# Delta rule in a decoder layer: substitution on 128 blocks of 16 rows instead of 64 of 32, one more doubling by products, one DMA per head each way, and other assumed durations in the planner

## The chip, the cores and the metric

The kernel runs on one core of one Trainium2 chip. The metric is the device time in microseconds of one execution on that core, as the median of several runs. TensorE is called PE in the profile, VectorE DVE, ScalarE ACT, GpSimd POOL and SyncE SP; PEld is TensorE's loading of weights, and SPq is the queue in which SP issues its DMAs.

## The reference

One layer of a decoder: a SwiGLU feed-forward network, a mixer of two head groups, a cross-attention to 256 memory tokens, and a second feed-forward network, over 512 tokens of width 1024, all in float32. The change is in the second head group of the mixer, the gated delta rule (4 heads of 128). Cut to what matters:

```python
L = where(strict, einsum('bhncd,bhnsd->bhncs', k_beta, k) * decay, 0.0)
A = L + eye(CHUNK)
u = triangular_solve(A, v_beta, left_side=True, lower=True)
w = triangular_solve(A, k_beta * exp(g)[..., None], left_side=True, lower=True)
attn_intra = einsum('bhncd,bhnsd->bhncs', q, k) * decay

def step(state, xs):                       # over the chunks
    w_c, u_c, qd_c, a_c, kt_c, gl_c = xs
    v_new = u_c - w_c @ state
    o = qd_c @ state + a_c @ v_new
    state = state * exp(gl_c) + kt_c.T @ v_new
    return state, o
```

The kernel works with chunks of 128 tokens, four per head, which give the same output. So for each head and chunk it needs the inverse of a unit lower triangular matrix I + L of 128 rows; T is that inverse, X its transpose.

## The kernel before

The feed-forward networks and projections are products of a [128 x 512] moving operand; every float32 weight block comes by DMA as `raw` (three buffers), ScalarE writes its high part `wh`, VectorE or GpSimd its low part `wl` (four buffers each), and TensorE makes three products of the parts. These are the "wide products" with `xt` and `wh` or `wl` in their names. In the mixer GpSimd makes the low part of every second block.

The order in which the engines issue is not the order of the code. The class `Issue` keeps every instruction with what it reads and writes, gives each an assumed duration (`add`, lines 119 to 183), and at the end (`settle`, line 226) places them on their engines, forwards and backwards by turns, the most urgent of those ready first. Each engine and SP's queue then issue in that order. Every instruction is recorded in one helper, so the profile shows one line, L270, for nearly all, and the names of tiles tell them apart.

The delta rule runs in these steps. The gates (`gw`, `yd`, `gc`) are worked out by token on VectorE, from a transpose of `zr` on TensorE. For each head the keys are convolved (`cy`, `cth`, `co`), transposed and multiplied (`kk`) to give `L` (lines 962 to 989). Then the diagonal blocks of 32 rows of all heads, 4 heads x 4 chunks x 4 blocks = 64, go through DRAM: `L` of a head is stored to `dl`, and four DMAs, one per chunk, load its blocks into `Lb` with a block to a partition. The substitution (lines 992 to 998) runs on 64 partitions for all heads at once, in `Tb`, which begins as the identity:

```python
for j in range(31):
    n = [64, 31 - j, j + 1]
    w_ = Wb[0:64, 0 : n[1] * n[2]].rearrange("p (r s) -> p r s", s=n[2])
    V.tensor_tensor(w_, Lb[:, j + 1 :, j : j + 1].to_broadcast(n), Tb[:, j : j + 1, 0 : j + 1].to_broadcast(n), ALU.mult)
    V.tensor_tensor(Tb[:, j + 1 :, 0 : j + 1], Tb[:, j + 1 :, 0 : j + 1], w_, ALU.subtract)
```

In `inverse` (line 1038), for each head, four DMAs store the blocks to `dt`, which holds zeros elsewhere, and one loads them as `T`; VectorE flips `T` to `X`. Small products then double the blocks twice, from 32 to 64 and from 64 to 128 rows: `L` times `X` into `Qs`, then `T` times `Qs` into `X` and, where the next doubling needs it, `T`. Then `qv` makes queries and values (`aT`, `vb`, `qe`), and `scan` runs over the four chunks. `PLAN` (line 29) orders these steps in the code, with `fox_values` (the values of the other head group, weights `wmn`) among them; it decides PSUM banks and buffers, and the planner's order follows from data and buffers. Behind the scans come the other head group's attention pairs.

## Time and profile before

| | |
|---|---|
| time of three runs | 1222.79, 1224.2, 1224.33 us; median 1224.2 |
| span of the profiled execution | 1222.4 us |
| TensorE busy | 1192.9 us, 98% |
| VectorE busy | 642.7 us, 53% |
| ScalarE, GpSimd busy | 493.0 us (40%), 128.6 us (11%) |
| chain of work that ended last | TensorE 87%, VectorE 7%, DMA 2% |
| mean granted clock of TensorE | 0.995 of full speed |

The span runs from the first instruction to the last of one execution; a run's time lies 1.8 us above it at the median, for what lies around it. Busy time is the union of an engine's instructions. The idle time of an engine is put down to what ended it. The granted clock is a share of full speed: 1.0 is 2.4 GHz, and where a stretch shows less, TensorE ran at 1.2 GHz for part of it.

### The profile page before, as it was taken

The page shows a single profiled execution, that of the slowest core. Times are in us where ns is not written, and L with a number is a line of the kernel's source. Part 1 is how long each engine was busy: PE and PEld are TensorE (multiplying, and loading weights), DVE is VectorE, ACT ScalarE, POOL GpSimd, SP SyncE. Part 2 cuts the span into 40 slices and gives each one's busy share as a digit, 9 for nine tenths or more (in the row PEclk, how much of TensorE's full clock was granted, in tenths as well). Part 3 has the DMA queues.
Part 4 walks back from the last instruction along what each step waited for, and adds up shares of the span by engine and source line. Part 5 has one row for each costly group of instructions (what it writes and reads, how often), then busy time and mean ns, then how long its engine had stood idle before and what let it go on. Part 6 is the DMA issues. An engine that isn't in the chain of part 4 may idle for free.

```text
span 1222.4 us, 15630 instructions
## 1 busy us (share of the span) xinstructions
PE 1192.9 (98%) x6078; PEld 1002.6 (82%) x6078; DVE 642.7 (53%) x1152; ACT 493.0 (40%) x1024; POOL 128.6 (11%) x121
## 2 busy tenths in 40 slices
PE   7999999999999899899999999999999999999997
PEld 7888888888888687788787888888988888888886
DVE  5655455442327979469975744546634334342323
ACT  5323223222226564368974644435422323222221
POOL 1000000000001432222020442012000000000000
PEclk9999999999999999999999999999999999999999
DMA  5332322333333231211214253222432332333321
GB/s 192 122 100 90 103 88 102 103 103 104 109 101 104 87 113 57 91 54 54 73 60 164 91 181 118 79 67 65 125 103 88 102 97 93 104 107 100 102 71 69
DMA packets 41753, 120.32 MB, mean 98 GB/s; under 512 B 9424, under 2 KB 9680, under 8 KB 41680
## 3 DMA queue, kind: packets, MB, share of 16 engines
q1 hardware_dynamic: 41168, 119.20, 30.9%
q8 instruction: 47, 0.77, 0.3%
q0 software_dynamic: 512, 0.13, 0.1%
q14 instruction: 26, 0.21, 0.1%
HBM read 114.73 MB, written 4.46 MB: 98 GB/s over the span
## 4 chain that ended last, share of the span: by engine, by line
PE 87%; DVE 7%; DMA 2%; issue 2%; ACT 2%; SPq 0%; POOL 0%; DVEq 0%; POOLq 0%; ACTq 0%
PE psum L270 87%; DVE Wb L270 1%; DVE Tb L270 1%; DMA mr<-in_mem_dram 1%; DVE wl L270 1%; DVE gw L270 1%; DMA raw<-in_wkvk_dram 1%; DVE co L270 1%; DVE xn L270 1%; DVE cy L270 0%; SPq L270 0%; DMA h<-in_x_dram 0%; DVE smalls L270 0%; DVE pt L270 0%; DVE h L270 0%
## 5 line engine op out<-in xcount | busy, mean ns | idle before, releaser
L270 PE MATMUL psum<-xt,wh 128*128 128x512 f32 (+1 forms) x2064 | 599.4, 374 | 0.3 <-ACT wh L270 0.2
L270 PEld LDWEIGHTS psum<-xt,wh 128*128 128x128 f32 x2064 | 373.6, 190 | 63.5 <-ACT wh L270 0.5
L270 ACT ACTIVATE wh<-raw 128x1024 fp32r<-128x1024 f32 (+1 forms) x202 | 213.0, 1056 | 526.0 <-PE psum L270 293.3
L270 PE MATMUL psum<-xt,wl 128*128 128x512 f32 (+1 forms) x1016 | 376.6, 375 | 0.8 <-DVE wl L270 0.7
L270 DVE TENSOR_TENSOR wl<-raw,wh 128x1024 fp32r<-128x1024 f32 (+1 forms) x176 | 216.3, 1230 | 275.8 <-ACT wh L270 275.2
L270 PEld LDWEIGHTS psum<-xt,wl 128*128 128x128 f32 x1016 | 190.9, 190 | 32.7 <-DVE wl L270 1.2
L270 PE MATMUL psum<-wh,hh 128*128 128x512 f32 x352 | 137.1, 390 | 0.0
L270 PE MATMUL psum<-wl,hh 128*128 128x512 f32 x352 | 137.1, 390 | 0.0
L270 PE MATMUL psum<-wh,hl 128*128 128x512 f32 x352 | 137.0, 389 | 0.0
L270 POOL TENSOR_TENSOR smalls<-smalls,mhalf 128x1 f32<-128x1 f32 (+1 forms) x38 | 26.5, 700 | 789.8 <-ACT smalls L270 784.0
L270 PEld LDWEIGHTS psum<-wh,hh 128*128 128x128 f32 x352 | 66.1, 188 | 13.8
L270 PEld LDWEIGHTS psum<-wh,hl 128*128 128x128 f32 x352 | 66.1, 188 | 13.6
L270 PEld LDWEIGHTS psum<-wl,hh 128*128 128x128 f32 x352 | 66.1, 188 | 13.6
L270 POOL TENSOR_TENSOR wl<-raw,wh 128x1024 fp32r<-128x1024 f32 x26 | 63.7, 2450 | 120.8 <-ACT wh L270 110.2
L270 PE MATMUL psum<-wh,xt 128*128 128x512 f32 x128 | 43.5, 409 | 0.4 <-DVE q L270 0.4
L270 DVE SCALAR_TENSOR_TENSOR hv<-s,psum 128x512 f32<-128x512 f32 x22 | 15.1, 688 | 53.7 <-PE psum L270 53.5
L270 DVE TENSOR_TENSOR tu<-psum,rb 128x512 f32<-128x512 f32 x22 | 15.2, 692 | 53.4 <-PE psum L270 53.3
L270 DVE TENSOR_TENSOR fg<-psum,gbc 128x512 f32<-128x512 f32 x32 | 22.0, 688 | 37.1 <-ACT u L270 37.1
L270 DVE TENSOR_TENSOR tg<-psum,rb 128x512 f32<-128x512 f32 x22 | 15.2, 692 | 44.5 <-PE psum L270 44.5
L270 ACT ACTIVATE u<-psum 128x512 f32<-128x512 f32 x32 | 19.0, 593 | 41.4 <-PE psum L270 41.4
L270 ACT ACTIVATE hh<-hv 128x512 fp32r<-128x512 f32 x44 | 27.4, 623 | 16.2 <-DVE hv L270 16.2
L270 DVE TENSOR_TENSOR hl<-hv,hh 128x512 fp32r<-128x512 f32 x44 | 30.1, 685 | 1.5 <-ACT hh L270 1.5
(232 smaller groups left out, 1431.3 us busy)
## 6 DMA issues: line engine op xcount, KB each, us to landing
raw<-in_f2gu_dram SPq DMA_DIRECT2D x44, 512.0 KB
raw<-in_f1gu_dram SPq DMA_DIRECT2D x43, 512.0 KB
raw<-in_f1d_dram SPq DMA_DIRECT2D x22, 512.0 KB
raw<-in_f2d_dram SPq DMA_DIRECT2D x22, 512.0 KB
raw<-in_wmt_dram SPq DMA_DIRECT2D x21, 512.0 KB
gbc<-in_gains_dram SPq DMA_DIRECT2D x16, 256.0 KB
raw<-in_wmn_dram SPq DMA_DIRECT2D x8, 512.0 KB
raw<-in_wout_dram SPq DMA_DIRECT2D x8, 512.0 KB
```

What stands on the lines that cost most here:

```text
L270: r = call(*args, **kw)
```

## The change

The blocks of the substitution have 16 rows, 128 of them, one on each partition, and it has 15 steps. A new doubling from 16 to 32 rows by products comes first: for each head 16 products `L` times `X`, a mask (`low16`, new columns of the constant `cr`) on the way from PSUM, 16 + 12 products with `Qs`, and seven subtractions on VectorE. The blocks of a head move with one DMA each way instead of four, in a layout of the DRAM buffers by chunks, with runs of 64 bytes instead of 128. `Lb` and `Tb` have 256 columns instead of 1024, `Wb` has a tile of its own, and there are 54 slots instead of 51. In the planner's assumed durations a float32r product costs 10.7 ns more, a float32 product on at most 32 rows half as much, and a `tensor_tensor_scan` 2.04 ns a column. Comments are gone as well, so the helper's line is now L273.

```diff
-NSLOT = 51
+NSLOT = 54
...
-            cost = max(size * passes * 0.41667, cols * 0.8333) + 2.6
+            cost = max(size * passes * 0.41667, cols * 0.8333) + (13.3 if passes == 1 else 2.6)
+            if passes == 4 and rows <= 32:
+                cost /= 2
...
-            cost = 68 + size * (6.3 if op == "reciprocal" else 0.521 if single else 1.042) + 61 * scalars
+            each = {"reciprocal": 6.3, "tensor_tensor_scan": 2.04}.get(op, 0.521 if single else 1.042)
+            cost = 68 + size * each + 61 * scalars
...
-    NB = 32 * S + 32
+    NB = 16 * P + 16
+    NC = 8 * NB
     def rows_of(buf):
-        return buf.rearrange("b x -> (b x)")[0 : P * S].rearrange("(p q) -> p q", q=S)
-    def blocks_of(buf, c):
-        return buf[:, 0 : 32 * S].rearrange("b (r q) -> b r q", q=S)[:, :, c * P : c * P + 32]
+        return buf.rearrange("c (p q) -> p c q", q=P)[0:P]
+    def blocks_of(buf):
+        flat = buf.rearrange("c x -> (c x)").rearrange("(i x) -> i x", x=NB)
+        return flat[:, 0 : 16 * P].rearrange("i (r q) -> i r q", q=P)[:, :, 0:16]
...
-        Q.dma_start(rows_of(dl[hh]), L)
-        for c in range(NT):
-            p0 = 16 * hh + 4 * c
-            Q.dma_start(Lb[p0 : p0 + 4], blocks_of(dl[hh], c))
+        Q.dma_start(rows_of(dl[hh]), by_chunk(L))
+        Q.dma_start(Lb[32 * hh : 32 * hh + 32], blocks_of(dl[hh]))
...
-    for j in range(31):
-        n = [64, 31 - j, j + 1]
-        w_ = Wb[0:64, 0 : n[1] * n[2]].rearrange("p (r s) -> p r s", s=n[2])
+    for j in range(15):
+        n = [P, 15 - j, j + 1]
+        w_ = Wb[:, 0 : n[1] * n[2]].rearrange("p (r s) -> p r s", s=n[2])
...
-        for c in range(NT):
-            p0 = 16 * hh + 4 * c
-            Q.dma_start(blocks_of(dt_[hh], c), Tb[p0 : p0 + 4])
+        Q.dma_start(blocks_of(dt_[hh]), Tb[32 * hh : 32 * hh + 32])
         T = u(s="T", ring=gr)
-        Q.dma_start(T, rows_of(dt_[hh]))
+        Q.dma_start(by_chunk(T), rows_of(dt_[hh]))
...
+        quarters = [slice(32 * i, 32 * i + 32) for i in range(4)]
+        qp = pg()
+        for c in range(NT):
+            for b in quarters:
+                mm(qp[b, 32 * c : 32 * c + 32], ck(L, c)[b, b], ck(X, c)[b, b], start=True, stop=True)
+        V.tensor_tensor(c3(Qs[:, 0:P]), c3(qp[:, 0:P]), low16[:, None, :].to_broadcast([P, NT, 32]), ALU.mult)
+        xp = pg()
+        for c in range(NT):
+            for b in quarters:
+                mm(xp[b, 32 * c : 32 * c + 32], ck(T, c)[b, b], Qs[b, 32 * c : 32 * c + 32], start=True, stop=True)
+            for b in quarters[0:3]:
+                mm(xp[b, P + 32 * c : P + 32 * c + 32], Qs[b, 32 * c : 32 * c + 32], ck(T, c)[b, b], start=True, stop=True)
+        for i, b in enumerate(quarters):
+            V.tensor_tensor(c3(X)[b, :, b], c3(X)[b, :, b], c3(xp[:, 0:P])[b], ALU.subtract)
+            if i < 3:
+                V.tensor_tensor(c3(T)[b, :, b], c3(T)[b, :, b], c3(xp[:, P : 2 * P])[b], ALU.subtract)
```

The change moves instructions on every engine. Three places show it; the numbers in the names tell buffers apart.

TensorE at the first product with X, before. `wh_4046` and `wh_4076` are weights of the values of the other head group:

```order
L270 MATMUL psum<-wh_4046,xt_2564 128x512
L270 MATMUL psum<-wh_4046,xt_2563 128x512
L270 MATMUL psum<-wl_4047,xt_2563 128x512
L270 MATMUL psum<-wh_4046,xt_2564 128x512
L270 MATMUL psum<-X_3692,L_3092 32x32 x4
L270 MATMUL psum<-wh_4076,xt_2563 128x512
L270 MATMUL psum<-wl_4077,xt_2563 128x512
L270 MATMUL psum<-wh_4076,xt_2564 128x512
```

And the same place after; `wh_3928` and `wh_3968` are the query and value weights of the last head:

```order
L273 MATMUL psum<-xt_2563,wl_3929 128x512
L273 MATMUL psum<-cm_2736 128x512
L273 MATMUL psum<-ao_3012,ao_3008 128x128 x4
L273 MATMUL psum<-xt_2561,wh_3968 128x512
L273 MATMUL psum<-X_3787,L_3141 32x32 x16
L273 MATMUL psum<-xt_2562,wh_3968 128x512
L273 MATMUL psum<-xt_2561,wl_3969 128x512
L273 MATMUL psum<-xt_2561,wh_3968 128x512
L273 MATMUL psum<-Qs_3789,T_3785 32x32 x4
L273 MATMUL psum<-T_3785,Qs_3789 32x32 x2
L273 MATMUL psum<-X_3645,L_3092 32x32 x13
```

The first product with X stood behind three of the four blocks of the other group's values; now it stands ahead of all four and inside the last head's projections, and two heads' small products follow each other.

VectorE from the end of the substitution to the flips of `T`, before:

```order
L270 TENSOR_TENSOR Wb_3048<-Lb,Tb 64x31
L270 TENSOR_TENSOR Tb<-Tb,Wb_3048 64x31
L270 TENSOR_TENSOR wl_4374<-raw_4371,wh_4373 128x1024
L270 STREAM_TRANSPOSE X_3692<-T_3690 128x512
L270 STREAM_TRANSPOSE X_3785<-T_3783 128x512
```

And after:

```order
L273 TENSOR_TENSOR Wb<-Lb,Tb 128x15
L273 TENSOR_TENSOR Tb<-Tb,Wb 128x15
L273 TENSOR_TENSOR wl_4071<-raw_4068,wh_4070 128x1024
L273 SCALAR_TENSOR_TENSOR co_3568<-cth_3562,cy_3560 128x512
L273 SCALAR_TENSOR_TENSOR cy_3600<-psum,cw,cy_3600 128x511
L273 TENSOR_TENSOR aT_3528<-psum,Dt_3517 128x512
L273 SCALAR_TENSOR_TENSOR cy_3600<-psum,cw,cy_3600 128x510
L273 STREAM_TRANSPOSE X_3787<-T_3785 128x512
L273 STREAM_TRANSPOSE X_3645<-T_3643 128x512
```

Five instructions, not one, stand between the last step and the first flip.

SP's queue on the way back, before; `raw` from `in_wmt` are weights of the attention pairs:

```order
L270 DMA raw_4329<-in_wmt_dram 128x1024
L270 DMA raw_4371<-in_wmt_dram 128x1024
L270 DMA raw_4568<-in_wmt_dram 128x1024
L270 DMA dt_3036<-Tb 4x32x32 x4
L270 DMA dt_3037<-Tb 4x32x32 x4
L270 DMA dt_3038<-Tb 4x32x32
L270 DMA T_3690<-dt_3036 128x512
L270 DMA dt_3038<-Tb 4x32x32 x3
L270 DMA T_3783<-dt_3037 128x512
L270 DMA dt_3039<-Tb 4x32x32 x4
L270 DMA raw_4610<-in_wmt_dram 128x1024
```

And after:

```order
L273 DMA raw_4128<-in_wmn_dram 128x1024
L273 DMA dt_3037<-Tb 32x16x16
L273 DMA dt_3036<-Tb 32x16x16
L273 DMA dt_3039<-Tb 32x16x16
L273 DMA dt_3038<-Tb 32x16x16
L273 DMA T_3785<-dt_3037 128x4x128
L273 DMA T_3643<-dt_3036 128x4x128
L273 DMA raw_4481<-in_wmt_dram 128x1024
L273 DMA raw_4523<-in_wmt_dram 128x1024
L273 DMA raw_4720<-in_wmt_dram 128x1024
```

Nine stores stood ahead of the first load of `T`, now four do, and the weights of the attention pairs moved from ahead of the stores to behind the loads.

## Rows read from the trace of the kernel before

**Rows 1.** The page, busy time by engine: share of the span, instructions.

```profile
PE 1192.9 (98%) x6078; PEld 1002.6 (82%) x6078; DVE 642.7 (53%) x1152; ACT 493.0 (40%) x1024; POOL 128.6 (11%) x121
```

**Rows 2.** TensorE in time: start, us, operation [idle before, what ended it].

```profile
410.80 1.08 PE L270 MATMUL psum<-ident,yd 128*128 128x128 f32 x4 [4.05 <-DVE smalls L270]
...
463.13 0.49 PE L270 MATMUL psum<-cm 128*128 128x512 f32 x1 [2.63 <-ACT vb L270]
...
502.32 0.52 PE L270 MATMUL psum<-X,L 32*32 32x32 f32 x8 [3.28 <-DVE X L270]
```

**Rows 3.** Stretches: length, PE, PEld, DVE, ACT, POOL busy, granted clock, DMA.

```profile
396.00:501.55 105.55, 95.10 (x482) 77.86 (x481) 90.89 (x182) 56.15 (x147) 36.76 (x24) 0.97 0.27 82
396.00:410.80 14.80, 10.75 (x75) 9.76 (x75) 14.33 (x28) 7.55 (x19) 7.08 (x4) 0.99 0.43 133
464.00:470.00 6.00, 6.00 (x23) 4.82 (x23) 5.90 (x11) 3.95 (x9) 1.10 (x1) 0.72 0.13 11
502.00:506.00 4.00, 3.68 (x15) 2.54 (x15) 0.97 (x2) 0.53 (x2) 0.60 (x1) 0.57 0.64 180
...
502.30:544.00 41.70, 41.64 (x402) 34.07 (x402) 23.01 (x63) 23.50 (x84) 7.21 (x9) 0.96 0.27 84
```

**Rows 4.** Stretches, the instructions with Wb alone: length, DVE busy, clock, DMA.

```profile
440.00:500.00 60.00, 29.96 (x62) 0.97 0.22 66
```

**Rows 5.** VectorE in time: three steps of the substitution, the last one with it.

```profile
449.72 0.21 DVE L270 TENSOR_TENSOR Tb<-Tb,Wb 64x60 f32<-64x60 f32 x1
...
457.39 2.46 DVE L270 TENSOR_TENSOR Wb<-Lb,Tb 64x207 f32<-64x207 f32 x1
...
492.53 2.41 DVE L270 TENSOR_TENSOR Tb<-Tb,Wb 64x31 f32<-64x31 f32 x1
```

**Rows 6.** GpSimd in time, at the second of those steps.

```profile
457.11 2.50 POOL L270 TENSOR_TENSOR wl<-raw,wh 128x1024 fp32r<-128x1024 f32 x1
```

**Rows 7.** TensorE in time: wide products one behind another.

```profile
497.06 0.39 PE L270 MATMUL psum<-wl,xt 128*128 128x512 f32 x1
...
497.74 0.39 PE L270 MATMUL psum<-wl,xt 128*128 128x512 f32 x1
```

**Rows 8.** Groups by form, 396 to 502 us: busy us, mean ns | idle before.

```profile
L270 DVE TENSOR_TENSOR wl<-raw,wh 128x1024 fp32r<-128x1024 f32 x8 | 10.1, 1264 | 0.0
...
L270 DVE SCALAR_TENSOR_TENSOR co<-cth,cy 128x512 f32<-128x512 f32 x11 | 9.3, 844 | 3.7 <-ACT cth L270 3.7
...
L270 DVE SCALAR_TENSOR_TENSOR cy<-psum,cw,cy 128x511 f32<-128x511 f32 x11 | 8.2, 745 | 1.8 <-ACT cth L270 1.7
```

**Rows 9.** The chain that ended last, 492 to 512 us: start, us, what.

```profile
494.96 0.27 SPq L270
...
498.87 2.65 DMA T<-dt
...
501.55 0.72 DVE X L270
```

**Rows 10.** SP's queue in time: a store of L, a load that waits.

```profile
428.07 0.33 SPq L270 DMA_DIRECT2D dl<-L  x1
...
430.42 0.67 SPq L270 DMA_DIRECT2D Lb<-dl  x2
```

**Rows 11.** Groups by form, 502 to 544 us: the first doubling's products.

```profile
L270 PE MATMUL psum<-X,L 32*32 32x32 f32 x64 | 3.4, 196 | 3.3 <-DVE X L270 3.3
```

**Rows 12.** TensorE in time: two groups of small products.

```profile
527.06 0.40 PE L270 MATMUL psum<-xt,wh 128*128 128x512 f32 x1
527.39 0.43 PE L270 MATMUL psum<-X,L 32*32 32x32 f32 x8
527.75 0.50 PE L270 MATMUL psum<-xt,wh 128*128 128x512 f32 x1
...
528.80 0.21 PE L270 MATMUL psum<-X,L 32*32 32x32 f32 x1
...
528.91 0.32 PE L270 MATMUL psum<-X,L 32*32 32x32 f32 x5
```

More of the change, by code (lines that the diff above doesn't have):

```diff
@@ L304, in tile_decoder_layer @@
     crow: bass.AP,
-    cid32: bass.AP,
+    cid16: bass.AP,
     out: bass.AP,
@@ L728, in tile_decoder_layer @@
     identR, mstrict, minclT, mdiag = (cm[:, i * P : (i + 1) * P] for i in range(4))
-    cr = issue.tile(pool, [P, 11], F32, tag="cr", name="cr")
+    cr = issue.tile(pool, [P, 43], F32, tag="cr", name="cr")
     QK.dma_start(cr, crow)
@@ L748, in tile_decoder_layer @@
     sel = cr[:, 7:11]
+    low16 = cr[:, 11:43]
     w_first = [wblock(wmt[i]) for i in range(4)]
@@ L895, in tile_decoder_layer, with by_chunk @@
         move("m", r_, n_)
-    NB = 32 * S + 32
+    NB = 16 * P + 16
+    NC = 8 * NB
     def rows_of(buf):
-        return buf.rearrange("b x -> (b x)")[0 : P * S].rearrange("(p q) -> p q", q=S)
-    def blocks_of(buf, c):
-        return buf[:, 0 : 32 * S].rearrange("b (r q) -> b r q", q=S)[:, :, c * P : c * P + 32]
-    dl = [issue.tile(dram, [4, NB], F32, tag="dl", bufs=4, name=nm("dl"), grain=(0, 32)) for _ in range(GH)]
-    dt_ = [issue.tile(dram, [4, NB], F32, tag="dt", bufs=4, name=nm("dt"), grain=(0, 32)) for _ in range(GH)]
+        return buf.rearrange("c (p q) -> p c q", q=P)[0:P]
+    def blocks_of(buf):
+        flat = buf.rearrange("c x -> (c x)").rearrange("(i x) -> i x", x=NB)
+        return flat[:, 0 : 16 * P].rearrange("i (r q) -> i r q", q=P)[:, :, 0:16]
+    dl = [issue.tile(dram, [4, NC], F32, tag="dl", bufs=4, name=nm("dl"), grain=(0, NC)) for _ in range(GH)]
+    dt_ = [issue.tile(dram, [4, NC], F32, tag="dt", bufs=4, name=nm("dt"), grain=(0, NC)) for _ in range(GH)]
+    def by_chunk(t_):
+        return t_.rearrange("p (c q) -> p c q", c=NT)
     zb = u(s="zb")
@@ L910, in tile_decoder_layer @@
     for hh in range(GH):
-        Q.dma_start(rows_of(dt_[hh]), zb)
+        Q.dma_start(rows_of(dt_[hh]), by_chunk(zb))
     fr(zb)
-    Lb, Tb = (issue.tile(pool, [P, D], F32, tag=t_, name=t_, grain=(4, 1024))[0:64].rearrange("p (r s) -> p r s", r=32) for t_ in ("Lb", "Tb"))
-    Wb = u(s="Wb")
-    QK.dma_start(Tb, cid32.rearrange("p (r s) -> p r s", r=32))
+    Lb, Tb = (
+        issue.tile(pool, [P, 256], F32, tag=t_, name=t_, grain=(32, 256)).rearrange("p (r s) -> p r s", r=16)
+        for t_ in ("Lb", "Tb")
+    )
+    Wb = issue.tile(pool, [P, 64], F32, tag="Wb", name="Wb")
+    QK.dma_start(Tb, cid16.rearrange("p (r s) -> p r s", r=16))
     def banks(hh):
@@ L1066, in inverse @@
             for c in range(NT):
-                mm(xp[up, 32 * c : 32 * c + 32], ck(T, c)[up, up], Qs[up, 32 * c : 32 * c + 32], start=True, stop=True)
+                mm(xp[up, 32 * c : 32 * c + 32], ck(T, c)[up, up], Qs[up, P + 32 * c : P + 32 * c + 32], start=True, stop=True)
                 if i == 0:
@@ L1070, in inverse @@
                         xp[dn, P + 32 * c : P + 32 * c + 32],
-                        Qs[up, 32 * c : 32 * c + 32],
+                        Qs[up, P + 32 * c : P + 32 * c + 32],
                         ck(T, c)[up, up],
@@ L1460, in _consts @@
     cmask = np.concatenate([ident, mstrict, minclT, mdiag], axis=1)
-    crow = np.zeros((P, 11), np.float32)
+    crow = np.zeros((P, 43), np.float32)
     crow[:, 0:1] = np.where(r % 16 < 4, 1.0, -1.0)
@@ L1471, in _consts @@
         crow[32 * m, 7 + m] = 1.0
-    cid32 = np.ascontiguousarray(np.broadcast_to(np.eye(32, dtype=np.float32).reshape(1, 1024), (64, 1024)))
-    return cmask, crow, cid32
+    crow[:, 11:43] = (r % 32 < 16) & (np.arange(32)[None, :] >= 16)
+    cid16 = np.ascontiguousarray(np.broadcast_to(np.eye(16, dtype=np.float32).reshape(1, 256), (P, 256)))
+    return cmask, crow, cid16
 def kernel(**inputs):
@@ L1535 @@
     )
-    cmask, crow, cid32 = _consts(np)
+    cmask, crow, cid16 = _consts(np)
     arrs = dict(
@@ L1558 @@
         crow=crow,
-        cid32=cid32,
+        cid16=cid16,
     )
```

6 lines of the change are left out of this document (2 added, 4 removed).

## The prediction

> **What bounds the kernel now.** I read the page first. TensorE is busy for 98% of the span [rows 1], so the time is TensorE's work plus its waits (the few us before its first and behind its last product aside), and a change counts only by what it adds to that work or takes from those waits. The second view is TensorE's instructions in time, with the idle time ahead of each. From 400 to 503 us three rows carry waits of over 2 us: 4.05 us ahead of the gates' transposes, 2.63 us ahead of a mask product, and 3.28 us ahead of the first doubling product, which waits for X [rows 2]. The last two, 5.9 us, fall while the substitution runs or just behind it. The third view is the stretches. From 396.00 to 501.55 us, from the gates' transposes to the flip that makes the first X, VectorE is busy for 90.89 of 105.55 us and TensorE for 95.10; behind the last two waits the granted clock is 0.72 for 6 us and 0.57 for 4 us [rows 3]. At the lower of the two levels (1.2 instead of 2.4 GHz for part of each stretch) TensorE loses 6 x 0.28 = 1.7 us and 4 x 0.43 = 1.7 us, the second partly while idle, say 1.6. So the lateness of VectorE costs 5.9 + 3.3 = 9.2 us at these two places. This is what the change can reach there.
>
> Why is VectorE late? The substitution takes 29.96 us of it, 62 instructions [rows 4]. A step of 60 columns takes 0.21 us when undisturbed; one of 207 columns took 2.46 us [rows 5], and just then GpSimd had a low part of a weight to make, for 2.50 us [rows 6]. Seven such long steps, from the third to the very last at 492.53 us (2.41 us), hold about 9 of the 30 us.
>
> **The substitution.** 15 steps of two instructions replace 31, on blocks of at most 64 columns. I take 0.21 us each from the undisturbed step of 60 columns [rows 5]: 30 x 0.21 = 6.3 us. VectorE is relieved of 29.96 - 6.3 = 23.7 us. If the new steps meet GpSimd as often as the old did per instruction, 30/62 of the 9 us come back and it is 19.
>
> **What else moves ahead of or behind the first X.** The order lists say more than the diff, because the planner's costs are edited too. From the gates' transposes to the first product with X, TensorE had 288 wide products (512 columns) and 54 half as wide; now it has 193 and 11. Three wide products take 0.68 us [rows 7], 0.227 each, so X is wanted (95 + 43/2) x 0.227 = 26.4 us of TensorE's work earlier. Work for a wait at X thus moves behind it. VectorE, too, has less to do ahead of X: three low parts of weights, three "co" and four "cy" fewer, at 1.26, 0.84 and 0.75 us [rows 8], 9.3 us, less 1.2 us for an "at" and an "ao" that came forward: 8.1 us.
>
> **The way back through DRAM.** Now nine stores are issued from 494.96 us on before the load of T, which is issued at 498.87 and lands after 2.65 us; the flip begins at 501.55 [rows 9], 6.6 us behind the last step. After, four stores are issued, of all heads, and the load waits only for its own head's. A store of L was issued at 428.07 and the load that waits for it at 430.42 [rows 10], so I put 2.35 us to a store: 2.35 + 2.65 = 5.0 us, 1.6 us less. The runs are shorter (64 bytes instead of 128) and there are 512 of them in a store; that cost is not shown. I bound it by nothing and by a second 2.35 us, and take nothing, since 256 KB of T land in 2.65 us. Behind the last step five VectorE instructions now stand ahead of the flip, about 3.7 us of work that fits into these 5.0 us, where one weight of 1.2 us stood: 2.5 us more are hidden. What is queued behind this on SP: the weights for the attention pairs now stand behind the loads of T instead of ahead of the stores. By the order 119 wide products, 27 us of TensorE's work, still lie between X and the first of those weights, so I cost that at nothing; without that cover it is one load, of about 2.7 us.
>
> **Balance at X.** VectorE comes 23.7 + 8.1 + 1.6 + 2.5 = 35.9 us earlier, TensorE 26.4 us earlier. VectorE gains 9.5 us on it, just over the 9.2 us that were lost at the two places. I take both waits, with their low clock, as gone: -9.2 us. The bounds are 0 and -9.2.
>
> **The gates.** The 14.8 us from 396.00 hold 14.33 us of VectorE's work and 4.05 us of TensorE's waiting [rows 3]. The same chain of gate instructions is there after the change, two weights' low parts among them. The work that covers it is 11 half and 36 wide products instead of 53 and 18, three wide ones less: +0.7 us. Bounds: the wait goes (-4.05) or it grows by the 2.5 us that one more meeting with GpSimd costs [rows 6].
>
> **The added products.** Each head gets 16 + 16 + 12 = 44 products of 32 x 32, 176 in all. The trace has 64 records for 32 such instructions [rows 11], two each, so 352 records. Four of them on one row group, with nothing beside them, start 34 ns apart (8 records, the last (0.43 - 0.19) us behind the first). In a mixed group, 10 records start from 528.80 to 528.91, 12 ns apart, where those of other rows and columns run beside each other [rows 12]. The new ones go round four row groups, so I take 12 ns: 4.2 us. A group also costs something at its ends: from 527.06 to 527.75 us 0.69 us pass, of which a wide product takes 0.227 and the eight records 0.27; 0.2 us are left. The order has 19 groups where it had 10: 1.8 us. Together +6.0 us; bounds 4.2 and 352 x 34 ns + 1.8 = 13.8 us.
>
> The Trainium skill speaks against the 12 ns: "TensorEngine Tiling (Array Packing)", Gotcha 1, says that row tiles cannot use one PSUM bank at the same time, and the four row groups of the new products write one bank. In the rows, the products that ran beside each other were in different banks or in one row group, so no run here shows it. By that rule this term would be the 13.8 us.
>
> Edits with one answer: the eight VectorE instructions more per head (one mask, seven subtractions, each on 32 rows or 128 columns) are 32 in all, at about 0.25 us 8 us, spread over a stage behind X in which VectorE is busy for 23.01 of 41.70 us [rows 3]; the fewer SP issues, three more slots and the smaller tiles cost nothing on a path.
>
> **Sum.** -9.2 + 0.7 + 6.0 = -2.5 us on a span of 1222.4. The median of the runs is 1224.2, 1.8 us above that span, so the forecast is **1221.7 us**.
>
> **Rivals.**
> *The products go one after another.* Where four row groups share a bank, each record costs 34 ns and the term is 13.8 us: -9.2 + 0.7 + 13.8 = +5.3, **1229.5 us**, slower. For it speaks that no row shows two row groups in one bank at once; against it, that TensorE waits for VectorE between the groups in any case. It decides from (9.2 - 0.7 - 1.8 + 2.4)/352 = 26 ns a record on.
> *VectorE is late again.* The planner has no cost for a meeting with GpSimd, and it has spent the relief on moving X forward. If those 9 us fall on other instructions, the balance is 0.5 us instead of 9.5 and nearly all of both waits stays: -0.5 + 0.7 + 6.0 = +6.2, **1230.4 us**; if half of them do, half the gain stays, **1226 us**. For it: GpSimd's work ahead of X falls only by two weights and two additions. Against it: these meetings were with steps on SBUF alone, and many of the instructions that are left read PSUM.
> *The wait at the gates goes too*, since the costs of scans and wide products are now nearer to their rows: 4.75 us less than the sum, **1217 us**. Against it: those costs do not hold what makes this chain long.
> *Gain and price cancel*, as where half of the wait at X stays: **1224 us**.
> That the change would not do what it says is excluded by the order: 30 steps stand there, and X stands ahead of the fox values.
>
> **How the numbers follow.** A measurement of this kernel tells 0.2%, 2.4 us, from no change. The sum lies just at that edge. The forecast's own range is 1219 to 1224.5 and has 0.46, a good half of it beyond the edge. The gates' wait going has 0.14, the cancelling 0.14, VectorE late 0.15 (mostly slower), the products one after another 0.11. So faster has 0.30 + 0.14 = 0.44, the same 0.16 + 0.12 + 0.02 = 0.30, slower 0.26. With a tenth left out at either end the range is 1214 to 1230.
>
> **What would show it.** Right: no wait of over 1 us at the first doubling product, none at the mask products, and the clock at its upper level from 440 us on; the substitution at 6 to 8 us of VectorE; groups of new products at 12 ns a record; a wait of 4 to 5 us still at the gates' transposes. Wrong: a wait at X or at the first scan with a low clock behind it; products of the first doubling 30 ns apart; a time between the last step and the flip of over 6 us; or waits beyond 560 us that the new order makes.

## The result and the profile after

The changed kernel takes 1236.2 us (four runs, 1232.8 to 1237.9), the kernel before 1224.3 in the same session: a ratio of 1.0099, 95% interval 1.008 to 1.0118. It is slower by 12 us, where 1221.7 was forecast. Executions of one kernel, in one and the same order, differ by up to 13 us here, with the granted clock of the execution (of the kernel with the durations alone, below, four of ten took 1229 to 1230 us at a mean clock of 0.992 to 0.994, and six took 1236 to 1239 us at 0.985 or 0.986), so below the ratios count first, and profiles, which show one execution each, second. The profiled execution has a span of 1235.6 us and took 1237.5.

The page's busy times, to be held against [rows 1]:

```profile
PE 1203.4 (97%) x6430; PEld 1007.2 (82%) x6430; DVE 631.9 (51%) x1152; ACT 494.0 (40%) x1024; POOL 133.3 (11%) x121
```

TensorE has 10.5 us more of busy time and 352 records more; its waits rose by 2.8 us. To see how much of the busy time is low clock, I went through the span in stretches of 2 us and summed busy time times (1 - granted clock). What is left after this and the idle time is the work at full clock:

| kernel | span | idle | lost to the lower clock | work at full clock |
|---|---|---|---|---|
| before | 1222.4 | 29.5 | 4.7 | 1188.3 |
| changed | 1235.6 | 32.3 | 7.4 | 1196.0 |

Where in the program does the change fall behind? Two marks stand in every trace: TensorE's first transposes of normed rows (`ident,xn`) behind the mixer and its output, and the first ones behind the cross-attention. (The memory tokens are transposed some 30 us ahead of the first mark, under the same name; those are not meant.) TensorE in time, before:

```profile
680.82 0.60 PE L270 MATMUL psum<-ident,xn 128*128 128x128 f32 x4
...
845.22 0.60 PE L270 MATMUL psum<-ident,xn 128*128 128x128 f32 x4
```

and after:

```profile
688.24 0.60 PE L273 MATMUL psum<-ident,xn 128*128 128x128 f32 x4
...
858.89 0.60 PE L273 MATMUL psum<-ident,xn 128*128 128x128 f32 x4
```

7.4 us are lost up to the first mark, in the mixer and its output, and 6.3 us between the marks (170.7 us instead of 164.4), where the change touches no line at all but the planner's durations. Behind the second mark both kernels take 377 us.

The mixer first. TensorE's waits in time, to be held against [rows 2]:

```profile
412.87 1.12 PE L273 MATMUL psum<-ident,yd 128*128 128x128 f32 x4 [3.30 <-DVE yd L273]
...
461.82 0.66 PE L273 MATMUL psum<-ident,co 128*128 128x128 f32 x4 [1.45 <-DVE co L273]
...
467.13 1.16 PE L273 MATMUL psum<-co,co 128*128 128x128 f32 x8 [0.77 <-ACT vb L273]
...
474.62 0.26 PE L273 MATMUL psum<-Qs,T 32*32 32x32 f32 x8 [1.07 <-DVE Qs L273]
```

The stretches behind the first and the last of these (length, PE, PEld, DVE, ACT and POOL busy, granted clock, DMA), against [rows 3]:

```profile
412.00:418.00 6.00, 5.13 (x14) 4.11 (x15) 5.96 (x12) 1.15 (x2) 1.08 (x1) 0.50 0.29 87
474.00:480.00 6.00, 5.34 (x103) 4.46 (x104) 3.92 (x11) 1.83 (x5) 1.44 (x2) 0.72 0.33 90
```

The first product with X waits for nothing now, and the wait of 2.63 us at the mask product and that of 3.28 us at X are gone. But smaller ones stand at the same work, and the clock still falls, for longer at the gates.

Between the marks there is one long wait (and one of 1.00 us ahead of it, at 702.41 us). TensorE's last products on the memory keys ahead of it, and the wait:

```profile
708.25 0.28 PE L273 MATMUL psum<-mT,wl 128*128 128x256 f32 x1
708.37 0.28 PE L273 MATMUL psum<-mT,wh 128*128 128x256 f32 x1
...
713.26 1.12 PE L273 MATMUL psum<-ident,xn 128*128 128x128 f32 x4 [4.61 <-DVE xn L273]
```

and the stretch from there:

```profile
712.00:718.00 6.00, 4.74 (x22) 4.75 (x23) 3.85 (x5) 1.80 (x3) 0.65 (x1) 0.51 0.41 126
```

The same place in the kernel before, the wait and the stretch:

```profile
708.97 0.66 PE L270 MATMUL psum<-ident,xn 128*128 128x128 f32 x4 [1.86 <-DVE xn L270]
...
708.00:714.00 6.00, 5.03 (x42) 5.03 (x43) 4.03 (x5) 2.37 (x4) 0.36 (x1) 1.00 0.46 142
```

In the changed kernel TensorE has run out of products, waits 4.61 us for the last block's normed rows (1.86 us in the kernel before) and then runs for some 6 us at the lower of the clock's two levels (0.51, 1.2 GHz), where the kernel before had no low clock. These two things are the whole loss between the marks: by the same split, TensorE is idle there for 5.6 us instead of 2.1 and loses 2.8 us to the lower clock instead of nothing, while its work at full clock is 162.3 us in both.

### The profile page after: what moved, and what is told of

Its sections match the earlier page's. It is cut to its first block, busy times and chain, and to the rows that moved or that the text cites. A ratio compares the mean times of both kernels' runs of the same rounds, so it can differ in the third digit from the quotient of the medians.

```text
span 1235.6 us, 16314 instructions
## 1 busy us (share of the span) xinstructions
PE 1203.4 (97%) x6430; PEld 1007.2 (82%) x6430; DVE 631.9 (51%) x1152; ACT 494.0 (40%) x1024; POOL 133.3 (11%) x121
## 4 chain that ended last, share of the span: by engine, by line
PE 85%; DVE 6%; ACT 2%; DMA 2%; issue 2%; POOL 2%; SPq 0%; POOLq 0%; DVEq 0%; ACTq 0%
PE psum L273 85%; DVE wl L273 1%; ACT wh L273 1%; POOL wl L273 1%; DVE cy L273 1%; DVE co L273 1%; DMA dl<-L 0%; DVE gw L273 0%; DVE xn L273 0%; DVE p L273 0%; DVE Tb L273 0%; POOL smalls L273 0%; DMA T<-dt 0%; DMA raw<-in_f1gu_dram 0%; DVE pt L273 0%
## 5 line engine op out<-in xcount | busy, mean ns | idle before, releaser
L273 PE MATMUL psum<-xt,wh 128*128 128x512 f32 (+1 forms) x2064 | 598.0, 375 | 0.0
L273 PEld LDWEIGHTS psum<-xt,wh 128*128 128x128 f32 x2064 | 373.1, 190 | 63.2 <-issue 0.2
L273 ACT ACTIVATE wh<-raw 128x1024 fp32r<-128x1024 f32 (+1 forms) x202 | 212.9, 1055 | 514.6 <-PE psum L273 280.3
L273 PE MATMUL psum<-xt,wl 128*128 128x512 f32 (+1 forms) x1016 | 376.5, 375 | 0.0
L273 DVE TENSOR_TENSOR wl<-raw,wh 128x1024 fp32r<-128x1024 f32 (+1 forms) x176 | 215.3, 1224 | 281.6 <-ACT wh L273 280.6
L273 PEld LDWEIGHTS psum<-xt,wl 128*128 128x128 f32 x1016 | 190.8, 190 | 31.6
L273 PE MATMUL psum<-wh,hh 128*128 128x512 f32 x352 | 137.1, 390 | 0.0
L273 PE MATMUL psum<-wh,hl 128*128 128x512 f32 x352 | 137.0, 390 | 0.0
L273 PE MATMUL psum<-wl,hh 128*128 128x512 f32 x352 | 137.0, 389 | 0.0
L273 POOL TENSOR_TENSOR smalls<-smalls,mhalf 128x1 f32<-128x1 f32 (+1 forms) x38 | 28.0, 738 | 491.3 <-ACT smalls L273 482.7
L273 PEld LDWEIGHTS psum<-wl,hh 128*128 128x128 f32 x352 | 66.1, 188 | 13.7
L273 PEld LDWEIGHTS psum<-wh,hh 128*128 128x128 f32 x352 | 66.1, 188 | 13.6
L273 PEld LDWEIGHTS psum<-wh,hl 128*128 128x128 f32 x352 | 66.1, 188 | 13.6
L273 POOL TENSOR_TENSOR wl<-raw,wh 128x1024 fp32r<-128x1024 f32 x26 | 63.1, 2427 | 124.3 <-ACT wh L273 124.2
L273 PE MATMUL psum<-wh,xt 128*128 128x512 f32 x128 | 43.7, 405 | 0.0
L273 DVE TENSOR_TENSOR fg<-psum,gbc 128x512 f32<-128x512 f32 x32 | 22.0, 687 | 40.9 <-ACT u L273 36.9
L273 DVE SCALAR_TENSOR_TENSOR hv<-s,psum 128x512 f32<-128x512 f32 x22 | 15.1, 687 | 51.6 <-PE psum L273 51.3
L273 DVE TENSOR_TENSOR tu<-psum,rb 128x512 f32<-128x512 f32 x22 | 15.2, 691 | 50.9 <-PE psum L273 50.9
L273 ACT ACTIVATE u<-psum 128x512 f32<-128x512 f32 x32 | 19.0, 594 | 48.0 <-PE psum L273 47.9
L273 DVE TENSOR_TENSOR tg<-psum,rb 128x512 f32<-128x512 f32 x22 | 15.2, 691 | 42.4 <-PE psum L273 42.4
L273 POOL MEMSET yd<- 128x512 f32 x1 | 0.5, 527 | 324.9 <-PE psum L273 324.9
L273 ACT ACTIVATE hh<-hv 128x512 fp32r<-128x512 f32 x44 | 27.4, 623 | 16.4 <-DVE hv L273 16.4
```

What stands on the lines that cost most here:

```text
L273: r = call(*args, **kw)
```

## The experiments

The change has two parts that can be taken apart: the new blocks (with the products, the DMAs and 54 slots), and the three assumed durations, which are the 13.3 ns beside a product, the halved cost of products on 32 rows, and the scans. **Theory A:** the loss is in the order that the new durations make. **Theory B:** it is in the new blocks' products and waits. The later expectations split theory A: A1 is that the 13.3 ns lose their time at the late wait, because fewer products stand ahead of it as cover (the work that TensorE can do while it would otherwise wait); A2 is that any other order is some us better or worse by chance. For each run the ratio to the kernel before on the same chip is given with its interval, and the table behind them has the marks.

**The durations alone, on the old blocks.** In the kernel before:

```diff
-            cost = max(size * passes * 0.41667, cols * 0.8333) + 2.6
+            cost = max(size * passes * 0.41667, cols * 0.8333) + (13.3 if passes == 1 else 2.6)
+            if passes == 4 and rows <= 32:
+                cost /= 2
...
-            cost = 68 + size * (6.3 if op == "reciprocal" else 0.521 if single else 1.042) + 61 * scalars
+            each = {"reciprocal": 6.3, "tensor_tensor_scan": 2.04}.get(op, 0.521 if single else 1.042)
+            cost = 68 + size * each + 61 * scalars
```

> The kernel before (64 blocks of 32 rows, four loads and stores a head, 51 slots) with only the three assumed durations changed. Theory A, the order that the new durations make is what costs: about 1234 to 1238 us, with the longer wait for the normed rows behind 700 us (4 to 5 us, with a low clock behind it) there as in the changed kernel. Theory B, the blocks and products cost it: 1222 to 1226 us, and a wait of under 2 us behind 700 us.

Measured: 1237.1 us, 1.0082 (1.0057 to 1.0107). The durations alone cost what the whole change costs, but not at the same places: the wait for the normed rows is 2.79 us, less than the 4 to 5 expected, 3.5 us are lost between the marks and 9.1 us ahead of them, and 16.0 us go to the lower clock (4.7 in the kernel before).

**The blocks alone.** The changed kernel with these lines as before.

> The changed kernel with the three assumed durations as they were before. Theory A (order): 1220 to 1226 us, since the substitution is as short and the order is the old planner's; TensorE's busy time 3 to 6 us above before. Theory B (blocks and products): 1234 to 1238 us.

Measured: 1220.8 us, 0.9972 (0.9954 to 0.999). Theory B falls: the blocks, with all their products, are 3.4 us faster than the kernel before, close to the -2.5 of the prediction's sum. In its profile TensorE idles for 23.5 us, loses 3.4 to the clock and works 1191.9; its busy time is 2.4 us above that before, a little less than the 3 to 6 expected.

**Which of the three.** The changed kernel with only the 13.3 ns:

```diff
-            if passes == 4 and rows <= 32:
-                cost /= 2
...
-            each = {"reciprocal": 6.3, "tensor_tensor_scan": 2.04}.get(op, 0.521 if single else 1.042)
-            cost = 68 + size * each + 61 * scalars
+            cost = 68 + size * (6.3 if op == "reciprocal" else 0.521 if single else 1.042) + 61 * scalars
```

> The changed kernel with only the 13.3 ns for products of one pass kept, and the costs of 32-row products and of scans as before. Theory A with the 13.3 ns as the cause: within 3 us of the changed kernel, 1233 to 1239 us. Theory A with the halved small products or the scans as the cause: 1220 to 1229 us. Theory B: 1234 to 1238 us whatever the durations.

Measured: 1231.5 us, 1.0058 (1.0032 to 1.0084). Just outside every range, nearest to theory A with the 13.3 ns as the cause. The reverse, 2.6 with the other two new durations kept:

> The changed kernel with 2.6 ns beside every product instead of 13.3, the two other new durations kept. If the 13.3 ns is the whole cause: 1219 to 1224 us. If the halved small products and the scans cost 4 to 5 us of their own: 1224 to 1228 us.

Measured: 1223.9 us, 1.0007 (0.9994 to 1.0019). And the halving alone:

> The new blocks with the old durations but for the halved cost of products on 32 rows. The cover between the last two blocks of normed rows is 9.4 us as with the old durations. Theory A1: 1218 to 1224 us, since only the stage with the small products is placed otherwise. If the halving is what costs the 4 to 5 us that lie between the changed kernel and that with only the 13.3 ns: 1224 to 1227 us.

Measured: 1222.0 us, 0.9977 (0.9963 to 0.9991). So in these runs the new blocks stay at the kernel before's time or under it without the 13.3 ns, and with it they don't. That this does not hold for every order, the runs with other slots and constants show below.

**The late place.** The changed kernel with the old durations from the memory tokens on (a flag in `add`, set at that line). TensorE's order list is that of the changed kernel up to the mixer's output:

```diff
+    issue.old = True
     gkv = gain_bc(G_MEMKV)
```

> The changed kernel, with the old assumed durations only from the memory tokens on; TensorE's order list is that of the changed kernel up to the mixer's output, and behind it the last two blocks of normed rows have 9.4 us of products between them again instead of 4.9. Theory A1 (the lost cover behind the mixer costs its wait and the low clock behind it, 2.7 + 3.5 us): 6 us less than the changed kernel, 1227 to 1231 us, wait for the normed rows under 2 us, and the rest of the loss (5 us against the kernel before) stays in the mixer. If that wait costs nothing because another takes its place: 1233 to 1238 us.

Measured: 1228.5 us, 1.0034 (1.0019 to 1.0048), 7.6 us less than the changed kernel. TensorE at the last block's normed rows in this kernel:

```profile
713.39 0.66 PE L276 MATMUL psum<-ident,xn 128*128 128x128 f32 x4 [0.41 <-DVE xn L276]
```

and its stretch:

```profile
712.00:718.00 6.00, 5.59 (x48) 5.39 (x47) 3.90 (x6) 3.80 (x5) 3.40 (x2) 1.00 0.62 195
```

The normed rows come at the same microsecond, but the wait is 0.41 us and the clock stays up. The order lists say why: between the last two blocks of normed rows stand 78 products of 256 columns on the memory keys with the old durations, and 41 with the new ones, which put the other 37 behind. 37 x 0.12 us (their spacing in the rows above) are 4.4 us; 4.61 - 0.41 = 4.2 us was the wait. The converse, new blocks with the old durations up to that line and the new ones behind it:

> The new blocks with the old assumed durations up to the memory tokens and the new ones behind. The cover between the last two blocks of normed rows is 4.9 us of products again. If the two places add: 1220.8 + 7.6 = 1228 us (1226 to 1231), with a wait of about 4.6 us for the normed rows and a low clock behind it, and the mixer as with the old durations. If not: 1219 to 1224 us.

Measured: 1229.1 us, 1.0027 (1.0011 to 1.0044): 8.3 us above the blocks alone by the medians, 6.7 us by the ratios. The wait, in TensorE's rows of this kernel:

```profile
706.98 1.11 PE L276 MATMUL psum<-ident,xn 128*128 128x128 f32 x4 [4.60 <-DVE xn L276]
```

and the stretch around it:

```profile
705.00:710.00 5.00, 3.02 (x14) 3.02 (x15) 3.88 (x4) 1.19 (x2) 1.38 (x1) 0.66 0.60 194
```

Put in and taken out, on the new blocks this one place is worth 7 to 8 us. That is shown. (Against the kernel before, which has a wait of 1.86 us there, it is the 6.3 us between the marks.)

**Why does a truer duration make it worse?** With 13.3 ns a product of 256 columns is assumed at 120 ns, which is what the trace shows. But the chain beside it, the last block's sum, power and normed rows on VectorE and GpSimd, is assumed too short. VectorE in the changed kernel:

```profile
702.93 3.55 DVE L273 SCALAR_TENSOR_TENSOR h<-fg,smalls,h 128x512 f32<-128x512 f32 x2
...
710.32 3.54 DVE L273 SCALAR_TENSOR_TENSOR xn<-h,smalls,gbc 128x512 f32<-128x512 f32 x2 [0.44 <-POOL smalls L273]
```

GpSimd:

```profile
702.56 2.71 POOL L273 TENSOR_TENSOR wl<-raw,wh 128x1024 fp32r<-128x1024 f32 x1 [0.48 <-ACT wh L273]
...
708.89 1.40 POOL L273 TENSOR_TENSOR smalls<-smalls,mhalf 128x1 f32<-128x1 f32 x1 [3.61 <-ACT smalls L273]
710.32 2.34 POOL L273 TENSOR_TENSOR wl<-raw,wh 128x1024 fp32r<-128x1024 f32 x1
```

By the formula in `add` a pair of such VectorE instructions is 2 x 0.66 = 1.3 us and a power 0.47; the rows have 3.5 us for each pair, when GpSimd makes a low part of a weight at that moment, and 1.40. So the planner takes this chain for some 5 us shorter than it is. The Trainium skill, "SBUF — State Buffer", section "Who interferes with whom", has the reason for the 3.5: a VectorE instruction with two SBUF inputs and a GpSimd instruction that reads SBUF hold a shared pair of ports one after the other; the 3.54 from 710.32 on, beside the 2.34 from the same moment, agrees. The test: the changed kernel with longer chains.

```diff
+            if len(sizes[0]) - scalars == 2 and not psum:
+                cost *= 1.4
...
-            cost = 140 + size * 2.1 if size > 4 else 300 + 165 * size
+            cost = 140 + size * 2.1 if size > 4 else 600 + 165 * size
```

> The changed kernel, with 1.4 times the assumed duration for VectorE's instructions with two operands in SBUF, and 0.3 us more for each of GpSimd's powers; the trace has these at 0.87 to 0.96 us (assumed 0.66) and 0.71 us (assumed 0.47). Theory A1 with the cause that VectorE's chains are assumed too short beside products that are now assumed right: waits for normed rows under 2 us and 1216 to 1226 us. If the chains' durations do not matter: 1232 to 1240 us.

Measured: 1235.1 us, 1.0101 (1.0069 to 1.0133), a miss. Yet between the marks it takes 164.2 us instead of 170.7, as the kernel before does: the late loss is gone. Up to the first mark it lost as much (694.2 us instead of 688.2), above all at the mixer's first products, where TensorE now waits 2.38, 1.18 and 2.64 us from 379 to 386 us. Nor is the late loss gone for the reason that the theory gives. VectorE's sum and TensorE's wait in this kernel:

```profile
707.47 1.40 DVE L275 SCALAR_TENSOR_TENSOR h<-fg,smalls,h 128x512 f32<-128x512 f32 x2
...
714.06 0.66 PE L275 MATMUL psum<-ident,xn 128*128 128x128 f32 x4 [0.40 <-DVE xn L275]
```

The sum meets no low part of GpSimd here (1.40 us instead of 3.55), the power takes 0.54 us instead of 1.40, and from the start of the sum to the transposes 6.6 us pass instead of 10.3. Only six more products stand in between, 0.7 us. So the chain itself came out shorter, and that longer assumed durations bring the cover back is not shown. What the planner does with the 13.3 ns is not explained either: a product assumed 10% longer does not by itself turn 78 products into 41. The expectations' covers, 9.4 us at 2.6 ns, 9.0 at 3.2, 8.9 at 4.0, 5.2 at 8.0 and 4.9 at 13.3, show a step between 4 and 8.

**The size of the constant.** On the blocks alone, 4.0 and 8.0 ns for the 2.6:

> The new blocks with the old durations, but 4.0 ns instead of 2.6 ns beside each product of one pass. In the order list, TensorE has about as much work (memory keys) between the last two blocks of normed rows as with 2.6 ns, 8.9 us instead of 9.4. Theory A1 (the constant costs by taking that cover away, from some value between 4 and 8 on): 1217 to 1224 us, wait for the normed rows at 700 us under 1 us. Theory A2 (any change of a constant gives another order, by chance some us better or worse): anywhere from 1216 to 1236 us, with the waits in other places.

Measured: 1225.1 us, 1.0029 (1.0004 to 1.0055), just above theory A1's range and inside that of A2.

> The same with 8.0 ns. In the order list the cover between the last two blocks of normed rows is 5.2 us, as with 13.3 ns (4.9). Theory A1: a wait of 3 to 5 us there, with 3 us of low clock behind it, and 1225 to 1232 us. Theory A2: no relation to the constant, 1216 to 1236 us.

Measured: 1238.1 us, 1.0118 (1.0096 to 1.0141), above both ranges and no better than with 13.3. The step between 4 and 8 is there between the marks (162.8 and 167.2 us), but ahead of the first mark both are slower too, where theory A1 has nothing to say.

**Both halves of the program.** The old durations in the mixer alone, the new ones elsewhere:

> The changed kernel, with the old assumed durations only inside the mixer, from its first constant to the memory tokens. Theory A1, the losses of the two places add: what the mixer's order costs (some 9 us by the trace up to the memory tokens' flips) goes and the wait of about 4.6 us for the normed rows stays: 1225 to 1229 us. If the mixer's order costs nothing: 1233 to 1238 us.

Measured: 1231.9 us, 1.0058 (1.0037 to 1.0079): 4.3 us less than the changed kernel, less than the 7 to 11 that were expected, and the late wait is there (4.60 us).

**Is the mixer's part a matter of the durations at all?** Changes that mean nothing to the computation: 51 slots in the changed kernel, 51 slots in the blocks alone, 3.2 ns instead of 2.6 in the blocks alone, and the last two kinds on the old blocks (50 slots; 3.2 ns).

> The changed kernel with 51 slots instead of 54. If the slots hold nothing (as the prediction put it): within 3 us of the changed kernel, 1233 to 1239 us. If the three slots buy something: 1240 us or more. If the reuse of slots in another turn is what moved the order for the worse: 1222 to 1230 us.

Measured: 1238.2 us, 1.0111 (1.0091 to 1.0131), as if the slots held nothing.

> The new blocks with the old durations and 51 slots. If the gain is the blocks' own: 1219 to 1223 us. If it hangs on one order: 1223 us or more.

Measured: 1238.7 us, 1.0109 (1.0071 to 1.0147): the gain hangs on one order.

> The new blocks with the old durations, 3.2 ns instead of 2.6 beside each product of one pass, a change of 0.3% of a wide product's duration; the order differs in many rows, the late cover is 9.0 us. Theory A1 (the size of the constant counts): 1219 to 1223 us. Theory A2 (every other order is some us better or worse in the mixer): 2 to 10 us off 1220.8, so 1223 to 1231 us.

Measured: 1227.4 us, 1.0033 (1.0008 to 1.0058), as theory A2 has it.

> The kernel before with 3.2 ns instead of 2.6 beside each product of one pass. If any other order of the mixer costs some us, whatever the blocks: 1226 to 1240 us, with low clock for 5 us or more in the stretch from 450 to 560 us. If only the new blocks with their 352 more records of small products fall to the low clock so easily: 1221 to 1226 us.

Measured: 1221.7 us, 0.9977 (0.9966 to 0.9988), inside the second range for the time, though the first range's 5 us of low clock are in its profile too.

> The kernel before with 50 slots instead of 51. If any other order costs: 1226 to 1240 us, low clock for 5 us or more from 450 to 560 us. If only the new blocks do: 1221 to 1226 us.

Measured: 1233.0 us, 1.0063 (1.0045 to 1.0082), as if any other order costs.

So the order ahead of the first mark alone is worth 18 us on the new blocks (1220.8 to 1238.7) and 11 on the old (1221.7 to 1233.0). That is more than executions of one order scatter: the blocks alone took 1220.2 to 1226.1 us in ten executions, and 1232.5 to 1242.4 in four with 51 slots. The gain of the blocks alone, 3.4 us, lies within that: the old blocks reach 1221.7 in another order. What the bad ones of these orders share is low clock in the stage of the small products. The 51-slot kernel's stretches:

```profile
478.00:500.00 22.00, 20.48 (x147) 15.68 (x148) 7.29 (x24) 5.49 (x18) 1.08 (x1) 0.54 0.07 25
534.00:554.00 20.00, 19.93 (x139) 15.52 (x139) 4.12 (x15) 4.22 (x15) 0.00 (x0) 0.51 0.00 1
```

The same stretches of the blocks alone with 54 slots, which in the second one have only wide products left:

```profile
478.00:500.00 22.00, 21.02 (x308) 16.49 (x298) 11.42 (x34) 9.43 (x32) 3.46 (x2) 1.00 0.16 51
534.00:554.00 20.00, 20.00 (x117) 17.09 (x116) 12.19 (x33) 14.75 (x42) 3.76 (x3) 1.00 0.10 28
```

And the old blocks with 50 slots, where the first product with X waits 3.34 us at 501.44, and below that the kernel before, where it waits 3.28 us [rows 2] and as many small products stand in the stretch:

```profile
500.00:522.00 22.00, 20.56 (x149) 15.65 (x150) 5.73 (x15) 6.47 (x20) 2.35 (x1) 0.53 0.29 92
```

```profile
500.00:522.00 22.00, 19.64 (x189) 15.94 (x190) 10.30 (x28) 9.64 (x34) 2.34 (x1) 0.92 0.33 104
```

In these stretches TensorE is never idle for long; it works through the small products at the lower level. The clock falls at a wait for one of them or right behind it: of 1.04 us at 478.75 and of 0.59 us at 534.07 with 51 slots, of 3.34 us with 50. But in the blocks alone waits of 0.62 us at 481.53 and of 0.58 us at 521.90, at products of the same kinds, are followed by no low clock, and the kernel before is back at its upper level within 4 us [rows 3]. What keeps the clock down in one order and not in the other is not shown.

**The price of the added products.** The blocks alone, each of the 176 new products issued twice, the order otherwise the same:

```diff
+    def twice(*a):
+        mm(*a, start=True, stop=True)
+        issue.free = True
+        mm(*a, start=True, stop=True)
+        issue.free = False
```

> The new blocks with the old durations, and each of the 176 new products of 32 rows issued twice, in an otherwise unchanged order on TensorE; the output is the same. By the spacing in the trace of the changed kernel (some 8.5 ns a record, 352 more records) the copies take 3.0 us: 1222 to 1225 us. By the rival that row groups on one bank go one after another (34 ns a record): 12 us more, 1231 to 1235 us.

Measured: 1248.5 us, 1.0197 (1.0172 to 1.0222). Neither theory: 27.7 us more. The split of its span tells where: work at full clock 1193.8 us, 1.9 more than the blocks alone, idle 27.2 (+3.7), and 23.7 lost to the lower clock (+20.3). The copies themselves cost some 2 to 4 us (the blocks alone with 51 slots, which lose nearly as much to the clock, 22.9 us, without a copy, work 1190.0 us by this split); the rest is in two stretches behind two waits in TensorE's queue, the first of which is

```profile
486.77 0.28 PE L273 MATMUL psum<-X,L 32*32 32x32 f32 x4 [2.06 <-issue]
```

and the stretches:

```profile
488.00:504.00 16.00, 16.00 (x126) 11.26 (x126) 1.40 (x4) 3.71 (x11) 0.00 (x0) 0.51 0.01 2
536.00:560.00 24.00, 23.95 (x263) 18.37 (x261) 6.40 (x23) 5.25 (x18) 0.00 (x0) 0.51 0.01 2
```

Whether the waits of 2 us or the density of small products brought the clock down was not taken apart. As the order with 51 slots brings it down as far without them, the copies are not the only way to it.

**Four DMAs each way.** The blocks alone, but with a load and a store for every chunk of a head, as before:

```diff
-        Q.dma_start(Lb[32 * hh : 32 * hh + 32], blocks_of(dl[hh]))
+        for c in range(NT):
+            p0 = 32 * hh + 8 * c
+            Q.dma_start(Lb[p0 : p0 + 8], blocks_of(dl[hh])[8 * c : 8 * c + 8])
```

> The new blocks with the old durations, but one load and one store for each 128 rows of a head, four each way, as in the kernel before. The prediction gave the single ones 1.6 us on the way back, hidden in part: 1221 to 1224 us. If the way through DRAM is hidden: 1219 to 1222 us. If four transfers a head delay X: a wait at the first product with X of over 2 us, and 1224 to 1228 us.

Measured: 1224.7 us, 1.0003 (0.9991 to 1.0014), 3.8 us above the blocks alone. No wait at the first product with X is over 0.6 us in its trace, and its order differs in many rows; after the runs above this difference can't be put to the DMAs.

The profiled execution of each kernel: time of the first mark, time between the marks, lost to the lower clock. (With 3.2 and 4.0 ns on the new blocks, with the longer chains and with 3.2 ns on the old blocks this execution took 1235.2, 1228.6, 1240.2 and 1225.4 us, 3.5 to 7.8 us more than the kernel's median.)

| kernel | first mark | between | low clock |
|---|---|---|---|
| before | 680.8 | 164.4 | 4.7 |
| changed | 688.2 | 170.7 | 7.4 |
| durations alone (old blocks) | 689.9 | 167.9 | 16.0 |
| blocks alone | 678.8 | 162.8 | 3.4 |
| only the 13.3 ns | 681.5 | 170.2 | 3.8 |
| scans and halving | 679.3 | 162.9 | 1.7 |
| halving | 678.5 | 164.3 | 1.4 |
| late durations old | 687.6 | 162.8 | 4.6 |
| late durations new | 682.0 | 169.6 | 4.8 |
| mixer's durations old | 682.9 | 170.4 | 4.3 |
| longer chains | 694.2 | 164.2 | 12.8 |
| 3.2 / 4.0 / 8.0 ns | 693.1 / 686.7 / 690.9 | 162.2 / 162.8 / 167.2 | 15.2 / 8.3 / 12.8 |
| changed, 51 slots | 693.7 | 167.0 | 10.5 |
| blocks alone, 51 slots | 699.4 | 162.8 | 22.9 |
| products twice | 704.8 | 162.7 | 23.7 |
| four DMAs | 680.9 | 162.8 | 1.7 |
| old blocks, 3.2 ns / 50 slots | 683.7 / 690.6 | 162.1 / 162.8 | 10.0 / 16.1 |

The column between the marks is a clean one: 162.1 to 164.4 us wherever the constant there is 4 ns or less or the chains are taken longer, 167.0 to 170.7 wherever it is 8 or 13.3. The first column is not: it goes with the low clock, and that changes with any change of the order, and from one execution of an order to another.

## Why the prediction was wrong

**The step that failed** is what the sum leaves out. The order lists were read for what the edited durations do between the gates and X, and the forecast has no term for what they do anywhere else; "waits beyond 560 us that the new order makes" stands only at its end, as a thing that would make it wrong. There is such a wait, at 713.26 us. With its low clock it makes the 6.3 us that the changed kernel loses between the marks, and with the old durations there the kernel is 7.6 us faster. The list had it, as the profile had the wait of 1.86 us at that place: 37 products moved behind the wait that they covered. What then remains against the kernel before, 4 us, is the mixer's order, against the blocks alone some 8, and there no single wait holds it: from 386 us to the memory tokens' transposes (658 us, in the blocks alone 649) the changed kernel has 4.4 us more idle time, 1.2 of low clock and 3.6 us spread over TensorE's busy time. That last part could not be put to a place and stays open; of this size is also what a change of one slot does.

**The range failed with it.** 1214 to 1230 came from the bounds of the single terms, as if the order of the rest were given. Moves of one to three slots or of 0.6 ns changed these kernels by 2 to 18 us; a change that has the planner place everything anew needs a range of that width.

Point by point, of the terms:

*The substitution* was put at 6.3 us, or, if steps meet GpSimd as often as before, 4.4 us more. It takes (stretch, the instructions with Wb alone, as [rows 4])

```profile
440.00:470.00 30.00, 9.78 (x30) 1.00 0.36 85
```

with three long instructions among the thirty, two of which are (as [rows 5])

```profile
456.81 2.31 DVE L273 TENSOR_TENSOR Tb<-Tb,Wb 128x63 f32<-128x63 f32 x1
...
464.40 0.95 DVE L273 TENSOR_TENSOR Tb<-Tb,Wb 128x15 f32<-128x15 f32 x1
```

just when GpSimd has a low part (2.38 us from 456.65) and an addition (1.09 us from 464.23). The mechanism and the alternative were right, the value taken was the more favourable of the two.

*The waits at the mask product and X* should have gone with their low clock, -9.2 us. What stands there now is 1.45 + 0.77 + 1.07 us and 0.28 x 6 = 1.7 us of low clock, 5.0 us, so about half of it came. The flip that makes the first X starts at 470.83 us instead of 501.55, 30.7 us earlier where 35.9 were reckoned. The blocks alone have 1.72 + 0.36 + 0.62 us and 1.6 of low clock, 4.3 us: much the same. "None at the mask products" held nearly (0.77 us stand at their neighbour), the clock "at its upper level from 440 us on" did not.

*The gates'* wait stays, but at 3.30 us; 4.05 + 0.7 us, 4 to 5, was forecast. That its low clock would grow from some 1.4 to 2.6 us (5.13 us at 0.50) was not.

*The way back* was put at 5.0 us. The last step ends at 465.35, the loads of T go out from

```profile
465.37 1.92 SPq L273 DMA_DIRECT2D dt<-Tb  x4
467.40 1.24 SPq L273 DMA_DIRECT2D T<-dt  x2
```

and the flip starts at 470.83, 5.5 us behind the last step instead of 6.6 [rows 9].

*The added products* were put at 6.0 us. 352 more records are there, as counted. TensorE in time, a group of 56, against [rows 12]:

```profile
482.21 0.26 PE L273 MATMUL psum<-Qs,T 32*32 32x32 f32 x8
482.29 0.20 PE L273 MATMUL psum<-T,Qs 32*32 32x32 f32 x3
482.31 0.21 PE L273 MATMUL psum<-Qs,T 32*32 32x32 f32 x1
...
482.67 0.24 PE L273 MATMUL psum<-T,Qs 32*32 32x32 f32 x6
482.84 0.49 PE L273 MATMUL psum<-xt,wh 128*128 128x512 f32 x1
```

From 482.21 to the last six at 482.67 fifty of them start, one in 9 ns, on four row groups and one bank. The term by the split of the blocks alone is 1191.9 - 1188.3 = 3.6 us. Four other kernels with the new blocks and about as little low clock (3.8 to 4.8 us: only the 13.3 ns, late durations old, late durations new, mixer's durations old) work 1192.9 to 1195.6 us, which makes it 4.6 to 7.3 us, so 6.0 was of the right size. The rival "the products go one after another" is excluded; the Trainium skill's rule for it ("TensorEngine Tiling (Array Packing)", Gotcha 1) isn't borne out by these rows. What the price left out is that small products can come with a low clock: issued twice they cost 27.7 us. That they bring it down at their single number is not shown, since the old blocks fall as well (16.1 us lost with 50 slots).

*The rivals.* "VectorE is late again" gave a time near the right one, 1230.4, and half its waits are there, but it isn't why the kernel is slower: with the old durations the same VectorE work takes 1220.8 us. That a gain and a price cancel holds for the blocks. The side on which the time fell had a chance of 0.26, all of it from mechanisms inside the stage that the diff names.

The sum of the blocks' own terms, -2.5 us, is near the -3.4 measured without the new durations, but after the runs with other orders that is not shown to be more than one order's luck.

## What to carry to other kernels

When a change edits the costs of a planner that sets the order of a whole program, compare the order lists at every place where the profile before has a wait or one just covered, and count the products that cover it; here a list of 78 against 41 products was worth 7 to 8 us. A truer duration for one engine can lose time. That it does so because another chain's durations stay too short, so that two errors had covered each other, is argued here and not shown. And before the gain of a few us is put to an edit, try the old kernel in a few other orders (one slot, 0.6 ns): if that alone moves it by 8 us (1233.0 us with 50 slots, 1224.9 with 51), only what recurs in all orders, like the time between two marks, tells of the edit.

## What was unexpected of the hardware

Small products run beside each other on four row groups of one bank, 9 ns a record, where 34 were feared. And in the stage where they are mixed with wide products, the granted clock can stay at its lower level for 16 to 24 us while TensorE is busy nearly all the time (19.93 of 20.00 us at 0.51 with 51 slots), with the same small products that run at 1.00 in another order of the same program (the blocks alone). Ahead of the first mark, low clock, from 1.4 to 22.9 us in all, is what separates the good orders of this kernel from the bad ones, more than its waits do (idle time 22.8 to 33.2 us). What decides which orders keep the clock up is not shown.
